# Weights split on GpSimd in narrower pieces, and one small product of a differential attention moved out of its loop

## The chip, the cores and the metric

The kernel runs on one core of a Trainium2 chip. The metric is the device time of one execution in microseconds (us). A core has five engines that work beside each other: TensorE (PE in the profile, its weight loads PEld), VectorE (DVE), ScalarE (ACT), GpSimd (POOL) and SyncE (SP), which here only issues DMAs. They meet through semaphores. SBUF is the memory on the chip that all of them use; PSUM is where PE writes its products.

## The reference

Four transformer layers run over 512 tokens of width 1024, batch 1, in float32: two of a first model (sparse attention with a convolution, then latent attention, each followed by an MLP of width 4096) and two of a second (a differential attention that also sees 256 context tokens, then an attention over a neighbourhood). Two things of it matter here. Every layer multiplies activations by large weight matrices (`h @ w_in`, `h @ w1` and so on). And the differential attention subtracts two softmaxes and normalises what comes out:

```python
    s = jnp.einsum('bqnd,bknd->bnqk', q, k).astype(F32) * scale
    p = jax.nn.softmax(s, axis=-1)
    p = p.reshape(bsz, n2 // 2, 2, nq, nk)
    w = p[:, :, 0] - lam * p[:, :, 1]
    o = jnp.einsum('bhqk,bkhe->bqhe', w.astype(v.dtype), v)
    ...
    o = rms_norm(o, subln_g) * (1.0 - lam_init)      # rms_norm adds EPS to the mean square
    (o.reshape(bsz, n, D_INNER) * jax.nn.silu(z)) @ w_out
```

## The kernel before

**Products in two parts.** PE multiplies in a float32 format of fewer bits (fp32r). To keep the reference's precision, each operand x is split into a rounded high part and the rest, x = hi + lo, and a product is three matmuls: hi x hi, hi x lo, lo x hi (`mm3`, lines 583, 584, 585). High parts are made by ACT (a copy into the rounded format), low parts by a subtraction on DVE or POOL (`sub_lo`, line 414, for activations).

**The stream of weights.** `WeightStream` passes all weights through SBUF in one order that `plan()` fixes: 355 units, most of them 128 partitions x 1024 columns, made of four blocks of 256 columns (`tm`, token-major products) or eight of 128 (`fmm`, feature-major). A block is what one step of the sum over the inner dimension uses. SP loads a unit into one of three raw buffers (line 264); `split` lets ACT make its high part (line 277) and POOL its low part (line 278) in one instruction each; a ring holds four split units. `tick` splits the next unit when the ring has room, and it is called after each group of products, so the order of the splits among POOL's other work is the order in which the program is written. Five units are split on DVE (`eng`). A matmul waits for the parts that it reads; an engine does its instructions in the written order.

**What else DVE and POOL do.** In the attentions, DVE turns scores in PSUM into masked scores with their extreme (L725, L2052, L2221), ACT exponentiates them into SBUF and sums each row, DVE divides (L735 in the causal attentions, L2232 in the neighbourhood attention), PE transposes the result. In layer 0 DVE also sums the index scores (L923). During the MLPs DVE forms the second model's modulation vector by long sums (L1267, `macc`). POOL makes low parts of activations (`hl`, L414), rotary products (L1701 to L1712), the gates (L1770) and, from its own queue, DMAs that copy the keys to the other 64 partitions (L1803).

**The differential attention** (`diff_run`) goes over 96 units (group of heads g, pair p, token tile t): 8 x 2 x 6. Unit by unit, one step apart: A forms two score tiles on PE; B adds the shift on DVE; E exponentiates on ACT, and each sum of a row lands in a small tile (`df_s0`, `df_s1`); Dm on DVE forms the factor of the second softmax, -lam x sum0 / sum1 (a reciprocal, L2072, and L2073), adds the second to the first (L2074) and writes EPS x sum0 squared into column t of the tile `oe` (L2077), for the softmaxes stay undivided and the norm's EPS must be scaled to match. T transposes, G multiplies by the values, and once for the six tiles of a pair Hn adds that column to the mean squares (L2111) and takes the root. The weight products of the next group run between these steps, with their splits.

Of the kernel before, what the change touches and what calls it, by code (L numbers as in the profile page):

```python
# [12 lines left out]
F32 = mybir.dt.float32  # L13
# [3 lines left out]
OP = mybir.AluOpType  # L17
# [8 lines left out]
EPS = 1e-6  # L26
# [220 lines left out]
class WeightStream:  # L247
# [20 lines left out]
    def split(s, eng=None):  # L268
        nc = s.nc
        u = s.halved  # L270
        s.load(u)
        key, nb, n = s.units[u]
        m = nb * n
        raw = s.raw.pop(u)
        hi = s.hi_pool.tile([128, UNIT], F32R, name="w_hi")
        lo = s.lo_pool.tile([128, UNIT], F32R, name="w_lo")
        nc.scalar.copy(hi[:, :m], raw[:, :m])  # L277
        (eng or nc.gpsimd).tensor_tensor(lo[:, :m], raw[:, :m], hi.bitcast(F32)[:, :m], OP.subtract)  # L278
        s.t[u] = lo, hi
        s.halved += 1  # L280
        s.load(u + s.ahead)
# [19 lines left out]
class Next:  # L301
    """Normalised input of a layer, feature-major in two parts, filled a pair of token tiles at a time."""

# [53 lines left out]
    def flush(s, n=4):  # L357
        """n of the four parts of the oldest pair's transposes."""
        parts = s.pend[0][1]
        for _ in range(min(n, len(parts))):  # L360
            parts.pop(0)()
        if not parts:
            s.pend.pop(0)
# [15 lines left out]
class Net:  # L379
# [22 lines left out]
    def psum(s, mm, tp=2, sp=0, s2=0):  # L402
        """The PSUM pools in force; a further call replaces them."""
        s.pctx.close()
        for n, b in (("tp", tp), ("mm", mm), ("sp", sp), ("s2", s2)):
            if b:
                setattr(s, n, s.pool_in(s.pctx, f"ps_{n}", b, space=PSUM))
# [179 lines left out]
    def tm(s, ps, units, xh, xl, tok, n, ks=range(8)):  # L587
        """Eight blocks of a token-major product, or those of ks."""
        blocks = [(u, b) for u in units for b in range(u[0].shape[1])]
        t = slice(tok, tok + 128)  # L590
        for k in ks:
            (wh, wl), b = blocks[k]
            s.mm3(ps, xh[:, k, t], xl[:, k, t], wh[:, b, :n], wl[:, b, :n], k == 0, k == 7)

    def fmm(s, ps, units, xh, xl, tok, n, c0=0, m=128, ks=range(8)):
        """The same with the features on the partitions."""
        blocks = [(u, b) for u in units for b in range(u[0].shape[1])]
        for k in ks:
            (wh, wl), b = blocks[k]
            s.mm3(ps, wh[:, b, c0:c0 + m], wl[:, b, c0:c0 + m], xh[:, k, tok:tok + n], xl[:, k, tok:tok + n], k == 0, k == 7)  # L600
# [10 lines left out]
    def rows_gemm(s, keys, lhs, evac, tail, npair, flush, wide_first=False, mid=None, k_first=False):  # L611
        """Token-major product over four 256-column chunks; the last two go pair of tiles by pair of tiles."""
        nc = s.nc
# [22 lines left out]
        def pair(i, c, us, free, between):  # L636
            """Two tiles, one weight unit after the other; the first unit is given back early where it is free."""
            ps = [s.mm.tile([128, 512], F32, name="mm")[:, :256] for _ in range(2)]
# [68 lines left out]
    def causal(s, units, qk, scale, mask, vs, pt, out, P, tmp, ofs, wide, fill, extra=lambda t: None):  # L707
        """Causal attention over (head, query tile) units; fill[t] holds the pieces of other work run in step t."""
        nc = s.nc
# [367 lines left out]
    def out_proj(s, name, order, lhs, M, ssp, rowt, sqp, make, gain, part=None, late=None):  # L1077
        """part: the first chunk's sum over the first unit, already formed."""
        nc = s.nc
# [501 lines left out]
    def tables2(s, pool, tmp):  # L1581
        """Rotary tables with the head gains folded in, the difference's factor and the output gain."""
        nc, io = s.nc, s.io
# [36 lines left out]
    def second(s, L, nx):  # L1620
# [135 lines left out]
        def gates_at(ts, g, chunks):  # L1756
            """z / (1 + exp(-z)), 128 columns at a time."""
            e = {}
# [254 lines left out]
    def diff_run(s, c):  # L2013
# [41 lines left out]
        def E(u):  # L2055
            g, p, t = u
            x = d[u]
            for j in range(2):
# [3 lines left out]
                ei[0] += 1  # L2062
                sm = s.sml.tile([128, 1], F32, name=f"df_s{j}")
                s.act(e, S, AF.Exp, bias=x["nb"][j], scale=-1.0, acc=sm)
                x["e"].append((e, sm))

        def Dm(u):
# [4 lines left out]
            nc.vector.reciprocal(rb, sb)  # L2072
            nc.vector.scalar_tensor_tensor(rb, sa, nlam, rb, OP.mult, OP.mult)  # L2073
            nc.vector.scalar_tensor_tensor(ea, eb, rb, ea, OP.mult, OP.add)  # L2074
            if t == 0:
                O[g, p] = ob.tile([128, 6, 128], F32, name="ob"), ob.tile([128, 6], F32, name="oss"), ob.tile([128, 6], F32, name="oe")
            nc.vector.scalar_tensor_tensor(O[g, p][2][:, t:t + 1], sa, EPS, sa, OP.mult, OP.mult)  # L2077

# [29 lines left out]
        def Hn(g, p):  # L2108
            o, ss, oe = O[g, p]
            v, y, a = [s.sml.tile([128, 6], F32, name=f"df_{k}") for k in "vya"]  # L2110
            nc.vector.scalar_tensor_tensor(v, ss, 1.0 / 128, oe, OP.mult, OP.add)  # L2111
            s.act(y, v, AF.Ln)
# [212 lines left out]
```

## Time and profile before

| | us |
|---|---|
| median of 3 runs | 3266.62 (3265.22 to 3267.99) |
| span of the profiled execution | 3260.0 |
| median of the runs over that span | 6.6 |
| PE busy | 3097.0 (95%) |
| DVE busy | 2143.7 (66%) |
| ACT busy | 1626.6 (50%) |
| POOL busy | 1527.3 (47%) |

The profile is of one execution. Its span goes from the first to the last instruction; the timed runs hold a few microseconds more around it. Busy time is the union of an engine's instructions. Durations are in us unless marked ns. An instruction that is held after it was issued shows a longer duration; one that waits for a semaphore shows idle time before it, and the profile names what ended that.

### The profile page before, as it was taken

The numbers are of one execution on the slowest core, as the hardware profiler recorded it, in microseconds if no ns is written. First come the engines' busy times: TensorE is split into PE (matmuls) and PEld (weight loads), VectorE is DVE, ScalarE is ACT, GpSimd is POOL, SyncE is SP. The second block draws the span as 40 slices with busy tenths as digits, with TensorE's granted clock in tenths as the row PEclk, the third lists the DMA queues.
The fourth block names the chain that finished last, engine by engine and source line by source line (L and its number), as shares of the span: only waits on it lengthen the run. The fifth ranks groups of instructions, "written<-read, shape, count | busy, mean of one in ns | idle before, by whom it ended". The sixth has DMA issues, their size and how long they took to land.

```text
span 3260.0 us, 59267 instructions
## 1 busy us (share of the span) xinstructions
PE 3097.0 (95%) x23124; PEld 2910.2 (89%) x23124; DVE 2143.7 (66%) x4332; ACT 1626.6 (50%) x3923; POOL 1527.3 (47%) x1344
## 2 busy tenths in 40 slices
PE   7999999998899999999999999998999999999889
PEld 7888889887788889889999999988999999999888
DVE  4885434466865354657777777778446777777775
ACT  4544533345765333455555555555235565555552
POOL 3433344434333444474654465443354554545544
PEclk9999999999999999999999999999999999999999
DMA  3122334432123343331222222212422323222324
GB/s 120 59 72 74 108 123 143 136 99 85 36 85 111 123 135 125 116 98 50 63 60 62 61 66 58 69 53 87 152 87 78 88 79 84 78 71 79 90 87 136
DMA packets 91012, 292.30 MB, mean 90 GB/s; under 512 B 18142, under 2 KB 23390, under 8 KB 87660
## 3 DMA queue, kind: packets, MB, share of 16 engines
q1 hardware_dynamic: 84028, 259.33, 24.7%
q0 software_dynamic: 5120, 25.17, 3.6%
q10 hardware_dynamic: 1584, 4.00, 0.4%
q8 instruction: 183, 3.00, 0.4%
q14 instruction: 97, 0.79, 0.1%
HBM read 244.38 MB, written 18.92 MB: 81 GB/s over the span
## 4 chain that ended last, share of the span: by engine, by line
PE 49%; DVE 11%; ACT 5%; issue 4%; POOL 3%; DMA 2%; SPq 0%; POOLq 0%; DVEq 0%; ACTq 0%
PE mm L583 12%; PE mm L585 12%; PE mm L584 12%; PE mm L2102 2%; ACT X L411 2%; POOL w_lo L278 2%; DMA KL<-KL 1%; PE s L2205 1%; PE tp L2244 1%; PE tp L2089 1%; PE mm L2259 1%; DVE s L2052 1%; PE mm L2253 1%; PE s L2206 1%; DVE X L735 1%
## 5 line engine op out<-in xcount | busy, mean ns | idle before, releaser
L278 POOL TENSOR_TENSOR w_lo<-w_raw,w_hi 128x1024 fp32r<-128x1024 f32 (+2 forms) x350 | 880.6, 2520 | 1033.8 <-ACT w_hi L277 1007.8
L583 PE MATMUL mm<-w_hi,hh 128*128 128x256 f32 (+3 forms) x2880 | 836.8, 291 | 7.8 <-ACT w_hi L277 2.5
L584 PE MATMUL mm<-w_lo,hh 128*128 128x256 f32 (+3 forms) x2880 | 817.0, 284 | 11.8 <-POOL w_lo L278 11.7
L585 PE MATMUL mm<-w_hi,hl 128*128 128x256 f32 (+3 forms) x2880 | 818.6, 284 | 2.8 <-POOL hl L414 2.4
L584 PEld LDWEIGHTS mm<-w_lo,hh 128*128 128x128 f32 x2880 | 548.0, 190 | 15.7 <-POOL w_lo L278 14.4
L583 PEld LDWEIGHTS mm<-w_hi,hh 128*128 128x128 f32 x2880 | 547.4, 190 | 16.0 <-ACT df_sq L411 8.5
L585 PEld LDWEIGHTS mm<-w_hi,hl 128*128 128x128 f32 x2880 | 546.2, 190 | 6.4 <-POOL hl L414 5.5
L277 ACT CAST w_hi<-w_raw 128x1024 fp32r<-128x1024 f32 (+2 forms) x355 | 366.5, 1036 | 206.0 <-PE mm L585 171.2
L583 PE MATMUL mm<-hh,w_hi 128*128 128x256 f32 (+1 forms) x1408 | 455.4, 323 | 3.0 <-DVE M L1088 2.8
L584 PE MATMUL mm<-hl,w_hi 128*128 128x256 f32 (+1 forms) x1408 | 448.2, 318 | 0.6
L585 PE MATMUL mm<-hh,w_lo 128*128 128x256 f32 (+1 forms) x1408 | 447.1, 318 | 1.2 <-DVE w_lo L278 1.2
L583 PEld LDWEIGHTS mm<-hh,w_hi 128*128 128x128 f32 x1408 | 266.0, 189 | 29.8 <-issue 5.2
L584 PE MATMUL mm<-w_lo,gh 128*128 128x256 f32 x1024 | 287.1, 280 | 1.4 <-POOL w_lo L278 1.4
L583 PE MATMUL mm<-w_hi,gh 128*128 128x256 f32 x1024 | 287.6, 281 | 0.0
L585 PE MATMUL mm<-w_hi,gl 128*128 128x256 f32 x1024 | 287.1, 280 | 0.1
L585 PEld LDWEIGHTS mm<-hh,w_lo 128*128 128x128 f32 x1408 | 265.7, 189 | 22.0 <-DVE w_lo L278 1.6
L584 PEld LDWEIGHTS mm<-hl,w_hi 128*128 128x128 f32 x1408 | 266.1, 189 | 21.3 <-DVE hl L345 1.7
L1267 DVE SCALAR_TENSOR_TENSOR macc<-modw,cg,macc 128x1024 f32<-128x1024 f32 x84 | 201.3, 2440 | 29.2 <-DMA modw<-in_mod 29.2
L584 PEld LDWEIGHTS mm<-w_lo,gh 128*128 128x128 f32 x1024 | 193.0, 188 | 1.9 <-POOL w_lo L278 1.6
L583 PEld LDWEIGHTS mm<-w_hi,gh 128*128 128x128 f32 x1024 | 193.2, 189 | 0.4
L585 PEld LDWEIGHTS mm<-w_hi,gl 128*128 128x128 f32 x1024 | 193.0, 188 | 0.5 <-DVE gl L414 0.5
L414 DVE TENSOR_TENSOR gl<-rsq,gh 128x512 fp32r<-128x512 f32 x64 | 45.6, 712 | 220.6 <-ACT gh L411 220.6
(372 smaller groups left out, 7089.0 us busy)
## 6 DMA issues: line engine op xcount, KB each, us to landing
w_raw<-in_w SPq DMA_DIRECT2D x336, 512.0 KB, 3.5
modw<-in_mod SPq DMA_DIRECT2D x24, 1024.0 KB, 5.8
KH<-KH POOLq DMA_DIRECT2D x32, 384.0 KB, 4.0
KL<-KL POOLq DMA_DIRECT2D x32, 384.0 KB, 5.0
xs<-X SPq DMA_DIRECT2D x12, 512.0 KB, 3.6
X<-xs SPq DMA_DIRECT2D x12, 512.0 KB, 6.7
yd<-ob SPq DMA_DIRECT2D x16, 384.0 KB, 2.3
X<-in_rpb SPq DMA_DIRECT2D x32, 192.0 KB, 3.7
```

What stands on the lines that cost most here:

```text
L277: nc.scalar.copy(hi[:, :m], raw[:, :m])
L278: (eng or nc.gpsimd).tensor_tensor(lo[:, :m], raw[:, :m], hi.bitcast(F32)[:, :m], OP.subtract)
L411: return s.nc.scalar.activation(out, in_, func, bias=bias, scale=scale, **kw)
L414: (eng or s.nc.vector).tensor_tensor(lo, x, hi.bitcast(F32), OP.subtract)
L583: mm(ps, ah, bh, start=first, stop=False)
L584: mm(ps, ah, bl, start=False, stop=False)
L585: mm(ps, al, bh, start=False, stop=last)
L735: nc.vector.tensor_scalar(d["P"][:, :d["n"]], d["P"][:, :d["n"]], rs, None, OP.mult)
L1267: nc.vector.scalar_tensor_tensor(acc[:, v], w[:, k2], cv, acc[:, v], OP.mult, OP.add)
L2052: nc.vector.tensor_tensor_reduce(S, S, s.zero.to_broadcast(list(S.shape)), nrq[:, h:h + 1], 3e38, OP.add, OP.min, nb)
L2089: nc.tensor.transpose(pt[:, k], ea[:, (k0 + k) * 128:(k0 + k + 1) * 128], s.ident)
L2102: nc.tensor.matmul(ps, x["w"][:, k], V[g][:, kb, p * 128:(p + 1) * 128], start=k == 0, stop=k == nk - 1)
```

## The change

The low half of a unit is made by POOL in several instructions of at least 256 columns each, whole blocks at a time: four for a unit of 4 x 256 or 8 x 128 columns, four of 276 for those of 1104. Units that DVE splits stay in one instruction.

In the differential attention the sum of the first softmax is written by ACT straight into column t of `oe`, which is allocated at the first exponential of a pair. L2077 leaves the loop; Hn squares all six columns and multiplies them by EPS in one instruction. The factor L2073 is formed by a tensor_scalar with two per-partition factors in place of a scalar_tensor_tensor. (Some docstrings became empty lines.)

```diff
@@ WeightStream.split
         nc.scalar.copy(hi[:, :m], raw[:, :m])
-        (eng or nc.gpsimd).tensor_tensor(lo[:, :m], raw[:, :m], hi.bitcast(F32)[:, :m], OP.subtract)
+        w = m if eng else n * max(1, 256 // n)
+        for c in range(0, m, w):
+            c = slice(c, min(m, c + w))
+            (eng or nc.gpsimd).tensor_tensor(lo[:, c], raw[:, c], hi.bitcast(F32)[:, c], OP.subtract)
@@ diff_run, E
-                sm = s.sml.tile([128, 1], F32, name=f"df_s{j}")
+                if j == 0 and t == 0:
+                    O[g, p] = ob.tile([128, 6, 128], F32, name="ob"), ob.tile([128, 6], F32, name="oss"), ob.tile([128, 6], F32, name="oe")
+                sm = s.sml.tile([128, 1], F32, name="df_s") if j else O[g, p][2][:, t:t + 1]
                 s.act(e, S, AF.Exp, bias=x["nb"][j], scale=-1.0, acc=sm)
@@ diff_run, Dm
             nc.vector.reciprocal(rb, sb)
-            nc.vector.scalar_tensor_tensor(rb, sa, nlam, rb, OP.mult, OP.mult)
+            nc.vector.tensor_scalar(rb, sa, rb, nlam, OP.mult, OP.mult)
             nc.vector.scalar_tensor_tensor(ea, eb, rb, ea, OP.mult, OP.add)
-            if t == 0:
-                O[g, p] = ob.tile([128, 6, 128], F32, name="ob"), ob.tile([128, 6], F32, name="oss"), ob.tile([128, 6], F32, name="oe")
-            nc.vector.scalar_tensor_tensor(O[g, p][2][:, t:t + 1], sa, EPS, sa, OP.mult, OP.mult)
@@ diff_run, Hn
+            nc.vector.scalar_tensor_tensor(oe, oe, EPS, oe, OP.mult, OP.mult)
             nc.vector.scalar_tensor_tensor(v, ss, 1.0 / 128, oe, OP.mult, OP.add)
```

## Rows read from the trace of the kernel before

**Rows 1.** The page: busy time by engine; the chain that ended last.

```profile
PE 3097.0 (95%) x23124; PEld 2910.2 (89%) x23124; DVE 2143.7 (66%) x4332; ACT 1626.6 (50%) x3923; POOL 1527.3 (47%) x1344
...
PE 49%; DVE 11%; ACT 5%; issue 4%; POOL 3%; DMA 2%; SPq 0%; POOLq 0%; DVEq 0%; ACTq 0%
```

**Rows 2.** Waits of PE: who waited for whom, us, times, longest.

```profile
PE s L2205 <- ACT X L411: 26.9, 39, 3.0
PE tp L743 <- DVE X L735: 20.2, 26, 1.5
...
PE mm L584 <- POOL w_lo L278: 13.1, 11, 2.2
PE tp L2244 <- DVE X L2232: 8.7, 5, 2.3
```

**Rows 3.** The core's span and its mean granted TensorE clock.

```profile
core 0: 3260.0 us, clock 0.991
```

**Rows 4.** POOL by line and shape: count; busy, mean ns; idle before.

```profile
L278 POOL TENSOR_TENSOR w_lo<-w_raw,w_hi 128x1024 fp32r<-128x1024 f32 x332 | 843.8, 2546 | 945.6 <-ACT w_hi L277 938.3 <-issue 2.5 <-PE tp L905 2.0
...
L1712 POOL TENSOR_TENSOR st<-X,X 128x256 f32<-128x256 f32 x64 | 47.8, 747 | 5.0
```

**Rows 5.** Timeline, 1386 to 1392.5: start, us, engine, line; idle time before.

```profile
1387.08 0.19 PEld L585 LDWEIGHTS mm<-w_hi,hl 128*128 128x128 f32 x1 [0.28 <-POOL hl L414]
...
1387.86 2.36 POOL L278 TENSOR_TENSOR w_lo<-w_raw,w_hi 128x1024 fp32r<-128x1024 f32 x1
...
1387.96 0.19 PEld L585 LDWEIGHTS mm<-w_hi,hl 128*128 128x128 f32 x1 [0.46 <-POOL hl L414]
...
1390.17 2.81 POOL L414 TENSOR_TENSOR hl<-nf_f,hh 128x256 fp32r<-128x256 f32 x4
...
1390.27 0.58 PE L584 MATMUL mm<-w_lo,hh 128*128 128x256 f32 x1 [1.50 <-POOL w_lo L278]
```

**Rows 6.** Two lines of DVE: ns minimum/median/maximum, first and last start.

```profile
L2077 DVE SCALAR_TENSOR_TENSOR oe<-df_s x96: 145/154/2392, 1459.8 to 2285.2; 128x1 f32<-128x1 f32 x96
...
L2232 DVE TENSOR_SCALAR X<-X,na_r x128: 486/554/2677, 2477.5 to 3185.5; 128x512 f32<-128x512 f32 x64, 128x640 f32<-128x640 f32 x64
```

**Rows 7.** DVE by line and shape: count; busy, mean ns; idle before.

```profile
L2052 DVE CUSTOM_DVE_ANT_0 s<-s,zero,nrq 128x768 f32<-128x768 f32 x128 | 127.3, 1022 | 3.9 <-PE s L2042 2.6
...
L2077 DVE SCALAR_TENSOR_TENSOR oe<-df_s 128x1 f32<-128x1 f32 x96 | 66.6, 693 | 0.0
...
L2073 DVE SCALAR_TENSOR_TENSOR df_rb<-df_s,nlam,df_rb 128x1 f32<-128x1 f32 x96 | 44.1, 459 | 3.5
...
L2072 DVE RECIPROCAL df_rb<-df_s 128x1 f32<-128x1 f32 x96 | 13.4, 140 | 97.9 <-ACT X L411 97.8
```

**Rows 8.** Timeline, 1671.5 to 1675.2: DVE and POOL in the differential attention.

```profile
1671.53 2.76 POOL L278 TENSOR_TENSOR w_lo<-w_raw,w_hi 128x1024 fp32r<-128x1024 f32 x1 [0.57 <-ACT w_hi L277]
...
1671.94 2.37 DVE L2077 SCALAR_TENSOR_TENSOR oe<-df_s 128x1 f32<-128x1 f32 x1
...
1674.24 0.47 POOL L1770 TENSOR_TENSOR SZ<-SZ,ge 128x128 f32<-128x128 f32 x1
```

**Rows 9.** Timeline, 3183 to 3189: POOL, DVE and PE in the neighbourhood attention.

```profile
3185.43 2.35 POOL L278 TENSOR_TENSOR w_lo<-w_raw,w_hi 128x1024 fp32r<-128x1024 f32 x1 [3.21 <-ACT w_hi L277]
...
3185.52 2.54 DVE L2232 TENSOR_SCALAR X<-X,na_r 128x512 f32<-128x512 f32 x1
...
3187.73 0.64 POOL L1770 TENSOR_TENSOR SZ<-SZ,ge 128x128 f32<-128x128 f32 x1
3188.20 0.63 PE L2244 MATMUL tp<-ident,X 128*128 128x128 f32 x4 [2.33 <-DVE X L2232]
```

**Rows 10.** Timeline, 404 to 411: DVE's long sums and a low half.

```profile
405.28 4.62 DVE L1267 SCALAR_TENSOR_TENSOR macc<-modw,cg,macc 128x1024 f32<-128x1024 f32 x2
...
405.66 3.17 POOL L278 TENSOR_TENSOR w_lo<-w_raw,w_hi 128x1024 fp32r<-128x1024 f32 x1 [2.84 <-ACT w_hi L277]
```

**Rows 11.** Timeline, 107 to 112: a DVE sum of layer 0.

```profile
108.82 2.19 DVE L923 SCALAR_TENSOR_TENSOR am<-relu,wi,am 128x384 f32<-128x384 f32 x1 [0.25 <-ACT relu L411]
```

## The prediction

> **What bounds the kernel now.** I read the page first. TensorE (PE) is busy 3097.0 of the 3260.0 us span, so it is the bound, and a change can only pay through the 163 us in which PE stands, or by making PE stand more [rows 1]. VectorE (DVE) holds 11% of the chain that ended last and POOL 3% [rows 1]: most of what PE waits for is made on DVE, little of it directly on POOL. The view of PE's waits then says where: behind DVE's softmax scalings (L735 20.2 us, L2232 8.7), behind exponentials that follow a DVE reduction (L2205, 26.9), and 13.1 us in 11 waits directly for a low half w_lo made on POOL [rows 2]. These are many short waits, none of them over 3.0 us in these rows. PE also lost a little to its clock: the mean granted clock is 0.991 [rows 3], so 0.009 x 3260 = 29 us of full-clock work was not granted. That time stands at the lower of the two levels (1.2 GHz) and comes after PE has stood.
>
> **POOL's cost of the pieces.** 332 of the 350 low halves are one instruction over 1024 columns, 2546 ns on average; 256 columns take 747 [rows 4]. So each instruction has a fixed part: (2546 - 747) / 768 = 2.34 ns a column leaves 747 - 256 x 2.34 = 148 ns. Behind one another, four instructions of 256 columns, of the same operation, took 2.81 us together [rows 5], against 2.36 for the whole unit just ahead of them. So each unit costs POOL 0.45 us more, 332 x 0.45 = 149 us, and POOL goes from 1527.3 us, 47% of the span [rows 1], to some 51%. It stays far from full. The low half in pieces is still one tile, but its readers need not wait for all of it: in rows 5 the tile hl is written by four POOL instructions, and PE waits for them one at a time (0.28 and 0.46 us at L585). I take it that w_lo is tracked the same way.
>
> **What the pieces free: DVE.** Many DVE instructions run far over their usual time, and the small ones tell why. L2077 works on one column and takes 154 ns at the median but 2392 at worst [rows 6], 693 on average [rows 7]. At 1671.94 it took 2.37 us: POOL had begun a w_lo at 1671.53, and L2077 ended as that w_lo did; the next POOL instruction was already issued at 1674.24 and cost its usual 0.47 [rows 8]. The same at 3185.52: L2232 (median of its line 554 ns) took 2.54 us behind the w_lo of 3185.43, and PE, which needed its result, stood 2.33 us [rows 9]. There DVE got in between two POOL instructions that followed one another: L1770 took 0.64 instead of 0.47 because DVE went first. L2052, which reads PSUM, took 1022 ns on average [rows 7] and shows no such holds. So a DVE instruction that reads or writes SBUF in this way waits for the end of the POOL instruction that is running, and POOL waits for DVE in turn: a w_lo that found DVE busy took 3.17 us [rows 10], and the second of two DVE sums then stood behind it, 4.62 us for both; it ended 1.1 us after the w_lo (405.28 + 4.62 - 405.66 - 3.17), about what one sum takes.
>
> With pieces DVE waits for the end of a piece, not of a unit. Each L2232 or L735 caught at the start of a unit waits up to 0.75 us, not 2.4. For the case in rows 9: the first piece would end 0.75 us after 3185.43, so DVE is done 1.6 us earlier, and PE's 2.33 us shrink to some 0.8.
>
> For the sum I followed every PE delay over 60 ns back (what released it, what that had waited for or stood behind on its engine, to the last matmul). The trail of 88 of them leads through 66 DVE instructions held by a w_lo; the first is L923 at 108.82 [rows 11], the last the L2232 of rows 9. Counting for each the shorter of PE's delay and the hold gives 48.5 us. Putting the end of the next piece (some 0.75 us after the start of the unit, then every 0.70, 2.81 / 4) in place of the unit's end leaves holds that give back 39.8 us of it. That is a ceiling for the step: the next DVE instruction of the same trail can be held again by the next piece (POOL goes first when DVE's next one follows directly, rows 10), and behind a shortened hold something else is late next, such as the exponential on ACT. I take 60%, **-24 us**; ends -48 and -5.
>
> In the multilayer perceptrons DVE's long sums (rows 10) gain nothing: two sums with a piece ahead of each wait no less in all than with one unit ahead of one of them once pieces and sums alternate, and POOL's unit grows to some 5 us (2.81 and two sums). PE does not stand there, so I cost it at zero; it would show as waits for w_lo if the four units in stock ran out.
>
> **The direct waits for w_lo.** In rows 5 PE stood 1.50 us for a w_lo of 2.36. Its first quarter would be there 1.6 us earlier, but the last 0.45 us later, and PE needs one quarter every 0.4 us (three products, at 3097.0 us for 23124 [rows 1] 0.13 us each) while POOL makes one in 0.7. PE would start early and then wait at each quarter, and the four blocks end about 0.5 us earlier. Eleven such waits: **-5 us**, ends -13 and +4.
>
> **What POOL's longer units delay.** Behind them in POOL's queue stand the gate products (L1770), the rotary products, the hl splits of the next layer (rows 5) and the two copies of the keys per group, issued from that queue. Each may start 0.45 us later. PE waits little for them, since 163 us of waits name them hardly [rows 2]; I charge ten places at 0.5: **+5 us**, ends 0 and +27 (the 3% of the chain that is POOL's, 98 us, stretched by 0.45/2.36 = 19%, gives +19; with DVE going first between pieces some +27).
>
> **The differential attention.** L2077 goes: 96 instructions, 66.6 us of DVE [rows 7], of which 96 x 0.154 = 15 us is work and the rest holds. Added are 16 instructions over six columns (as long as one column by their kind, 16 x 0.15 = 2.5 us). L2073 becomes one instruction with two per-partition factors. No row shows that form on one column: if it is never held and as short as L2072's reciprocals, 96 x (459 - 140) ns = 31 us of DVE go too; if it is held like L2073, nothing goes. I take the middle, as pieces shorten the hold to 0.25 either way. On PE nearly all of this is inside the 66 trails (12 go through L2077, 7 through L2073, about 9 us of delay together), since PE stands little in that stage; so 0 beside the -24, ends -4 and 0. The sum column that ACT now writes straight into the group's tile moves no instruction.
> The Trainium skill, SBUF — State Buffer, "Summary: rules for kernel authors", says that tensor_scalar can enter a mode that takes the pair of ports shared with GpSimd. By that rule the new factor is held as before; the sum would be 0 to 1 us higher. L2232, a tensor_scalar between SBUF tiles, agrees [rows 9]; for one column no run shows it.
>
> **Clock.** With a third of PE's stops shortened some of the stretches at the lower level should not come: **-3 us**, ends -12 and +3.
>
> **Sum** against the profiled execution: 3260.0 - 24 - 5 + 5 - 3 = 3233 us of span. The timed runs (median 3266.6) stand 6.6 us above that span, so 3240.
>
> **Rivals.**
> A, everything held comes free (48 + 13, 4 in the attention, 6 of clock, 5 lost): 3266.6 - 66 = 3201. For it: holds repeat group by group with the same length. Against: trails share later steps. With three quarters of it, 3217. Chance 0.12 for below 3222.
> B, the freed DVE time is off PE's path: other work is late next, a quarter of the ceiling is kept (-10) and POOL takes 6 back: 3262. For it: PE is already at 95%. Against: rows 9, where nothing stands between DVE and PE. Chance 0.14.
> C, slower: POOL becomes the late one where layers meet, around 1320 to 1440 us and 2400 to 2440, where PE already waits for w_lo behind hl splits [rows 5]. The 3% of the chain grows by 27 us with DVE let in between pieces, and DVE gives 8: 3286. It decides once a unit with its interruptions takes longer than PE needs for one. Against: POOL is idle half of the span. Chance 0.08.
> The Trainium skill, VectorE: DVE Perf Modes, "The TRN2 errata", advises tiles of 512 columns or more because each instruction pays a fixed part; it speaks of VectorE and ScalarE. It points to rival C; by rows 4 two pieces of 512 would cost POOL 0.15 us a unit and hold DVE 1.35 us at most.
> D, the change doesn't do what it says: POOL keeps going through its four pieces before DVE gets in. Then holds grow by 0.45 us, 66 x 0.3 = +20 less 4 in the attention: 3282. Against: rows 8 and 9. Chance 0.03.
>
> **Numbers.** Forecast 3240 with chance 0.63, its own range 3222 to 3256. 0.2% is 6.5 us, about what timing can tell from no change. The range 3214 to 3266 takes in most of A and B. Faster (below 3260): forecast, A and a third of B, 0.79; same: the rest of B and the top of the forecast's spread, 0.11; slower: C and D, 0.10.
>
> **What would show it.** Right: some 1370 POOL instructions on L281 of 0.7 us each; POOL busy near 1680 us (1527.3 and 149); the longest L2232 (then L2235) near 1.3 us instead of 2.68; DVE busy below 2000; PE's waits behind L735 and L2232 (then L738 and L2235) down by half; PE's busy time about the same and the span near 3233. Wrong: PE waits for w_lo above 13 us in total, holds on DVE still above 2 us, or DVE freed by 150 us with PE's waits unchanged.

## The result and the profile after

The change makes the kernel faster: 3242.5 us (median; 3240.7 to 3243.8) against 3267.3 before, ratio 0.9923, 95% interval 0.9909 to 0.9937. The forecast was 3240. The profiled execution took 3240.7 us with a span of 3238.6, where 3233 had been worked out. So a run stands some 2 us above its own span, as all runs on record do. Of the 6.6 us by which the sum went from span to time, the other 4.5 must come from the profiled execution of before having taken some 3262 us and not the median's 3266.6; so the span missed by 5.6 us where the time missed by 2.5, and two traces differ by 21.4 us where the medians differ by 24.8.

Busy time by engine and the chain that ended last, of the kernel after, as in [rows 1]:

```profile
PE 3097.3 (96%) x23124; PEld 2914.6 (90%) x23124; DVE 1930.0 (60%) x4252; ACT 1618.0 (50%) x3923; POOL 1741.3 (54%) x2376
...
PE 56%; DVE 6%; POOL 4%; ACT 4%; issue 3%; DMA 2%; SPq 0%; POOLq 0%; DVEq 0%; ACTq 0%
```

PE does the same work in the same busy time (3097.0 and 3097.3), so in sum the 21.4 us of span are time in which PE stood; stretch by stretch that is not so, as the tables below show. DVE lost 214 us and nearly half of its share of the chain; POOL gained as much, 214 us.

PE's waits after, as in [rows 2]:

```profile
PE s L2208 <- ACT X L414: 21.2, 33, 3.0
PE tp L746 <- DVE X L738: 16.0, 22, 1.5
...
PE mm L588 <- POOL hl L417: 5.6, 5, 2.3
PE mm L586 <- DVE ot L1957: 5.5, 3, 3.1
...
PE mm L587 <- POOL w_lo L281: 4.3, 11, 0.6
...
PE s L2044 <- DMA KH<-KH: 3.6, 1, 3.6
PE s L2208 <- DMA KH<-KH: 3.3, 1, 3.3
...
PE tp L2247 <- DVE X L2235: 1.5, 2, 0.8
```

The waits that the pieces were to shorten are shorter: 26.9 to 21.2, 20.2 to 16.0, 13.1 to 4.3 and 8.7 to 1.5 us. The forecast had L735 and L2232 together down by half; they went from 28.9 to 17.5, L735 by a fifth only. Four rows grew. In the kernel before they were:

```profile
PE mm L585 <- POOL hl L414: 2.4, 4, 1.0
...
PE s L2205 <- DMA KH<-KH: 2.2, 2, 2.0
...
PE mm L583 <- DVE ot L1954: 1.5, 2, 0.8
...
PE s L2041 <- DMA KH<-KH: 0.4, 1, 0.4
```

The growth behind hl and the copies of the keys (KH) has a place in the forecast, that behind the product's eviction L1957 (L1954 before) has none. The copy that PE's L2044 waited for is in layer 2 (near 1440 us), the one of L2208 in the last layer (near 3078 us).

What one hold became shows at the place of [rows 9]. POOL, DVE and PE in the timeline after:

```profile
3165.99 3.01 POOL L281 TENSOR_TENSOR w_lo<-w_raw,w_hi 128x256 fp32r<-128x256 f32 x4 [3.22 <-ACT w_hi L277]
...
3166.09 0.93 DVE L2235 TENSOR_SCALAR X<-X,na_r 128x512 f32<-128x512 f32 x1
...
3167.16 0.63 PE L2247 MATMUL tp<-ident,X 128*128 128x128 f32 x4 [0.70 <-DVE X L2235]
```

DVE comes in after the first of four pieces and is done in 0.93 us instead of 2.54; PE stands 0.70 us instead of 2.33. The forecast for this place was 1.6 us earlier and some 0.8.

POOL's pieces and two groups of DVE (by line and shape: count; busy, mean ns; idle before), and the minimum/median/maximum of the two lines that answer to [rows 6]:

```profile
L281 POOL TENSOR_TENSOR w_lo<-w_raw,w_hi 128x256 fp32r<-128x256 f32 x1336 | 1061.6, 826 | 802.3 <-ACT w_hi L277 780.2 <-PE mm L587 9.3 <-issue 5.6
...
L1270 DVE SCALAR_TENSOR_TENSOR macc<-modw,cg,macc 128x1024 f32<-128x1024 f32 x84 | 127.7, 1564 | 31.8 <-DMA modw<-in_mod 31.8
...
L2078 DVE TENSOR_SCALAR df_rb<-oe,df_rb,nlam x96: 272/273/276, 1450.7 to 2265.9; 128x1 f32<-128x1 f32 x96
...
L2235 DVE TENSOR_SCALAR X<-X,na_r x128: 485/554/1112, 2466.4 to 3166.1; 128x512 f32<-128x512 f32 x64, 128x640 f32<-128x640 f32 x64
```

A piece takes 826 ns on average, not the 700 of four undisturbed ones, since DVE gets in between. Four of them take 3.18 us (1061.6 / 334), against 843.8 / 332 = 2.54 for a whole unit in [rows 4]. So a unit costs POOL 0.64 us more and not 0.45; that is the difference between POOL's 1741 us and the 1680 of the forecast.

**Where along the program the time came from.** Both kernels issue 23124 matmuls in the same order, so the start of the n-th matmul can be subtracted between two traces. The table gives how much each kernel won (+) or lost on the kernel before in each stretch (bounds by the time of before, us). It also holds the experiments below.

```
             0-   320-  680-  900- 1340- 1400- 1480- 2280- 2360- 2480- 3080- 3160-   all
            320   680   900  1340  1400  1480  2280  2360  2480  3080  3160   end
after     +12.4  +0.4  -0.8  +2.2  -2.4  -3.9 +10.9  -5.9  -4.0 +11.5  -2.6  +3.7  +21.4
pieces    +11.1  +0.4  -0.9  +2.2  -2.4  -3.1 +10.1  -2.7  -4.1 +11.0  -4.5  +3.8  +20.7
attn       +1.6  +0.0  -0.6  +0.6  -0.2  +0.1  +7.8  -0.7  -0.0  +0.3  -0.5  +0.0   +8.5
meet whole +9.4  +0.4  -2.3  +2.3  -3.0  +0.7 +10.2  -0.3  -0.6 +10.9  -2.6  +3.7  +28.9
yraw ACT  +11.8  +0.4  -1.0  +2.3  -2.5  -3.9 +11.2  -5.9  -4.4 +11.1  -2.0  +2.6  +19.8
refill    +12.7  +0.4  -0.9  +2.3  -2.6  -3.5 +10.8  +1.7  +0.1 +12.2  -1.8  +3.7  +35.2
reversed   +8.5  -0.4  -0.1  +1.5  -3.9  -3.2 +11.0  -3.4  -4.4 +11.2  -4.6  +3.4  +15.6
512       +11.3  +0.2  -1.8  +1.6  -2.5  -2.9 +10.3  -2.9  +1.4 +11.2  -3.3  +2.7  +25.6
mlp whole +11.0  +0.1  +0.0  +1.9  -0.1  -5.2 +10.7  -5.6  -0.1 +10.7  -2.4  +3.4  +24.5
5th piece  +2.2  -1.1  -5.4  -1.1  -9.5 -10.2 +10.0  -7.7  -6.5  +0.6  -5.9  -3.0  -37.5
select     +9.7  +0.0  +2.2  +0.7  -0.2  -1.6  +9.9  -0.2  -0.7 +10.1  -5.0  +3.7  +28.6
sel 512   +11.3  +0.1  -0.2  +1.5  -0.6  +0.3  +9.1  -1.4  -2.2 +10.9  -2.8  +2.5  +28.4
sel no at  +8.7  +0.0  +2.5  +0.7  +0.8  +0.4  +9.2  +0.2  -3.1 +11.0  -1.5  +3.6  +32.5
```

Each row is one execution. Part of a row is time in which PE stood, the rest is PE's own busy time, which is longer where more of it ran at the lower clock. The second table takes PE's busy time out of both traces: by how much PE stood less (+) or more (-) than before in the same stretches, and the mean granted clock of a stretch in the two kernels.

```
             0-   320-  680-  900- 1340- 1400- 1480- 2280- 2360- 2480- 3080- 3160-   all
            320   680   900  1340  1400  1480  2280  2360  2480  3080  3160   end
after      +9.6  +0.3  +0.5  +1.0  -0.7  -3.0  +6.8  -4.0  -0.4  +9.9  -1.8  +3.6  +21.7
meet whole +9.1  +0.3  +0.8  +1.0  -0.8  +0.2  +4.9  -0.2  -0.6  +9.4  -2.5  +3.6  +25.3
refill     +9.9  +0.3  +0.6  +1.0  -0.9  -2.6  +6.8  +1.5  +0.2 +10.7  -1.9  +3.6  +29.1
reversed   +6.1  -0.2  +1.3  +0.4  -0.4  -2.1  +7.0  -3.0  -2.5  +9.7  -3.7  +3.5  +16.2
512        +9.9  +0.0  +0.2  +0.4  -0.2  -1.0  +6.6  -2.3  +0.3  +9.8  -1.0  +2.6  +25.5
mlp whole  +9.3  -0.0  -0.3  +0.6  +0.3  -3.0  +7.0  -3.0  +0.1  +9.0  -1.3  +3.3  +22.0
5th piece  +5.0  -1.0  -2.6  -1.4  -4.5  -6.8  +5.4  -4.8  -3.1  +1.4  -4.7  +1.2  -16.1
clock bef. 0.98  1.00  0.98  1.00  0.94  1.00  0.99  1.00  0.99  1.00  0.94  1.00  0.991
clock aft. 1.00  1.00  0.97  1.00  0.92  0.98  1.00  0.98  0.96  1.00  0.92  0.99  0.990
```

The change wins 41.1 us in six stretches and loses 19.6 us in the other six, 16.2 of them where one layer hands over to the next (1340 to 1480 and 2280 to 2480 us). That is twice the net result, and the experiments are about these two sums. PE's standing shows the same two sides, smaller: 31.7 us less in seven stretches, 9.9 us more in five, and in each of the five the clock also came out lower. So half of the loss, and a quarter of the gain, is PE's busy time. The five kernels with the same units before 320 us (after, pieces, meet whole, yraw ACT, refill) won from 9.4 to 12.7 us there, and stood less by 9.1 to 9.9: the standing repeats better than the total.

**Where the late transfers come from.** In the stretch 2280 to 2360 us PE waits for the product's eviction L1957, which on DVE stands behind the split of yraw, which waits for a load. SP's DMA issues, POOL and PE of the kernel after:

```profile
2319.76 1.52 SPq L1942 DMA_DIRECT2D yraw<-yd  x2
2325.44 4.39 SPq L264 DMA_DIRECT2D w_raw<-in_w  x2
2329.92 0.86 SPq L1942 DMA_DIRECT2D yraw<-yd  x2
...
2321.49 7.97 POOL L281 TENSOR_TENSOR w_lo<-w_raw,w_hi 128x256 fp32r<-128x256 f32 x8
...
2320.12 0.39 PE L586 MATMUL mm<-w_hi,hh 128*128 128x256 f32 x1 [2.07 <-DVE ot L1957]
2336.21 0.53 PE L586 MATMUL mm<-w_hi,yh 128*128 128x256 f32 x1 [3.09 <-DVE ot L1957]
```

The same place in the kernel before (18.7 us later on its clock):

```profile
2336.53 1.52 SPq L1939 DMA_DIRECT2D yraw<-yd  x2
2340.88 2.88 SPq L264 DMA_DIRECT2D w_raw<-in_w  x2
2344.24 1.99 SPq L1939 DMA_DIRECT2D yraw<-yd  x2
...
2338.27 5.13 POOL L278 TENSOR_TENSOR w_lo<-w_raw,w_hi 128x1024 fp32r<-128x1024 f32 x2
...
2350.53 0.39 PE L583 MATMUL mm<-w_hi,yh 128*128 128x256 f32 x1 [0.63 <-DVE ot L1954]
```

A load of w_raw needs a raw buffer, and a buffer is free when the unit in it has been split. Two units took POOL 5.13 us before and 7.97 after, with DVE's splits going in between. So the second load left SP only at some 2329.5 (the row of two that starts at 2325.44 ends at 2329.83), and the yraw load queued behind it left at 2329.92: 4.4 us later than the 2344.24 of before, set on the same clock (2344.24 - 18.7 = 2325.5). The 5.9 us lost in this stretch are 4.0 of standing and 1.9 of PE's busy time, at a granted clock of 0.98 instead of 1.00 after the stop of 3.09 us.

For the KH of layer 2 the queue is not the matter but, as I read it, the transfers beside it. Median issue to landing around the first group of layer 2, before (first fence) and after:

```profile
w_raw<-in_w SPq DMA_DIRECT2D x4, 512.0 KB, 3.8
KH<-KH POOLq DMA_DIRECT2D x2, 384.0 KB, 4.6
```

```profile
w_raw<-in_w SPq DMA_DIRECT2D x4, 512.0 KB, 6.3
KH<-KH POOLq DMA_DIRECT2D x2, 384.0 KB, 7.5
```

The first copy's issue before and after:

```profile
1445.14 0.75 POOL L1803 DMA_DIRECT2D KH<-KH  x1 [1.28 <-ACT KH L411]
```

```profile
1433.40 0.75 POOL L1806 DMA_DIRECT2D KH<-KH  x1
```

At this point the matmuls of the kernel after are 12.3 us ahead, so the copy left 0.6 us later against them (1433.40, and 1445.14 - 12.3 = 1432.84). And the group's two copies took 2.9 us longer at the median (7.5 and 4.6): the two loads of w_raw ahead of it had left SP 1.5 and 1.9 us later (at 1430.67 and 1433.48, before at 1441.51 and 1443.89), and the second ran together with it. That the load beside it is what slowed the copy is not shown by an experiment of its own; where the second load left some 1.3 us ahead of the copy again (meet whole and select), the first copy landed in 4.4 and 4.5 us.

### The profile page after: what moved, and what is told of

It reads as the page before. It is cut to its first block, busy times and chain, and to the rows that moved or that the text cites. A ratio compares the mean times of both kernels' runs of the same rounds, so it can differ in the third digit from the quotient of the medians.

```text
span 3238.6 us, 60338 instructions
## 1 busy us (share of the span) xinstructions
PE 3097.3 (96%) x23124; PEld 2914.6 (90%) x23124; DVE 1930.0 (60%) x4252; ACT 1618.0 (50%) x3923; POOL 1741.3 (54%) x2376
## 4 chain that ended last, share of the span: by engine, by line
PE 56%; DVE 6%; POOL 4%; ACT 4%; issue 3%; DMA 2%; SPq 0%; POOLq 0%; DVEq 0%; ACTq 0%
PE mm L586 14%; PE mm L588 14%; PE mm L587 14%; PE mm L2104 3%; POOL w_lo L281 3%; PE tp L2091 2%; PE s L2044 1%; DMA KL<-KL 1%; PE s L2045 1%; PE s L2208 1%; ACT X L414 1%; PE tp L2247 1%; PE mm L2262 1%; PE s L2209 1%; PE mm L2256 1%
## 5 line engine op out<-in xcount | busy, mean ns | idle before, releaser
L281 POOL TENSOR_TENSOR w_lo<-w_raw,w_hi 128x256 fp32r<-128x256 f32 (+2 forms) x1382 | 1100.6, 828 | 876.2 <-ACT w_hi L277 836.4
L2055 DVE CUSTOM_DVE_ANT_0 s<-s,zero,nrq 128x768 f32<-128x768 f32 (+1 forms) x192 | 158.7, 844 | 18.4 <-PE s L2045 15.7
```

The lines of the kernel that those rows point to most:

```text
L281: (eng or nc.gpsimd).tensor_tensor(lo[:, c], raw[:, c], hi.bitcast(F32)[:, c], OP.subtract)
L2055: nc.vector.tensor_tensor_reduce(S, S, s.zero.to_broadcast(list(S.shape)), nrq[:, h:h + 1], 3e38, OP.add, OP.min, nb)
```

## Experiments

Ratios are to the kernel before, run beside each. The change itself stands at 0.9923 (0.9909 to 0.9937), so a kernel differs from it surely only where the intervals part.

**The two parts alone.** First the pieces without the attention's edits, then these with whole units:

```diff
-        (eng or nc.gpsimd).tensor_tensor(lo[:, :m], raw[:, :m], ...)
+        w = m if eng else n * max(1, 256 // n)
+        for c in range(0, m, w): ...
```

> The kernel before with the pieces of 256 columns and nothing else of the change. Theory P (nearly all of the gain is the shorter holds): 3240 to 3246 us against 3267 before and 3242 for the whole change; L2077 (one column) stays but its mean falls from 693 ns to some 250. Rival Q (the attention's part carries a share of its own, the 9 us of PE delay that was traced through L2077 and L2073): some 3250 us. In both the four places where the changed kernel loses against the kernel before (near 1370, 1450, 2340 and 2465 us) lose again if the pieces make them.

> The kernel before with the differential attention's part alone, whole units of 1024 columns on POOL. Theory P: 3263 us (4 us less than 3267, at most 9, all between 1450 and 2250 us), the new factor's instruction still up to 2.4 us long at worst because a whole unit holds it. Rival Q: 3258 us. Neither expects a loss near 2340 or 2465 us, which the pieces are to make.

Measured: the pieces 3241.6 us, 0.9932 (0.9917 to 0.9947), as good as the whole change. The attention's part 3257.7 us, 0.9978 (0.9968 to 0.9988): 7 us (4 to 10 by the interval), nearer Q's 9 than P's 4. (The traced execution took 3253.3 us, so its total in the table is some 4 us high.) The pieces lose again at all four places near 1370, 1450, 2340 and 2465 us (-2.4, -3.1, -2.7 and -4.1), the attention's part at none (-0.7 at most): the pieces make these losses. P holds for the pieces, Q for the attention alone, and the parts don't add: between 1480 and 2280 us they win 10.1 and 7.8 us alone and 10.9 together. They remove the same stops: PE's waits there behind DVE's splits of the keys and queries (KL, QS) were 6.7 us before and are 1.4, 2.1 and 1.1 us with the pieces, the attention's part and both. The new factor's instruction in the kernel with whole units, and in the pieces alone the two lines that it replaces:

```profile
L2075 DVE TENSOR_SCALAR df_rb<-oe,df_rb,nlam x96: 272/273/277, 1457.0 to 2275.1; 128x1 f32<-128x1 f32 x96
```

```profile
L2080 DVE SCALAR_TENSOR_TENSOR oe<-df_s x96: 147/154/705, 1452.5 to 2267.9; 128x1 f32<-128x1 f32 x96
...
L2076 DVE SCALAR_TENSOR_TENSOR df_rb<-df_s,nlam,df_rb x96: 219/291/1573, 1451.3 to 2267.2; 128x1 f32<-128x1 f32 x96
```

The one instruction with two factors is never held, even by whole units (277 ns at most), where P expected up to 2.4 us. L2080 is the L2077 of before, which took 2392 ns at worst in [rows 6]; with pieces it takes 705, one piece. Its mean fell from 693 to 375 ns, not to the 250 that P expected.

**Whole units where layers meet.**

```diff
-        w = m if eng else ...
+        w = m if eng or 199 <= u < 203 or 259 <= u < 283 else ...
```

> The whole change, but 28 of 355 units are again formed in one instruction: v2:0, q2:1, all of o2 and all of layer 3 up to q3:1, those that POOL forms between 1417 and 1440 and between 2200 and 2460 us. Theory M: a unit in pieces is done 0.45 us later, or up to 2.8 us for two where DVE gets in between, so its raw buffer is free later, the next load of w_raw is issued later on SP, and it collides there with the copies KH and KL (PE waited 3.6 and 3.3 us for KH) or holds up the yraw loads queued behind it (PE waited 3.1 us behind L1957). Then three places that lost 4.4, 5.9 and 4.0 us are won back: 3242 - 14 = 3228 us, at worst half of it, 3235. Rival N: those losses come from DVE's new order or from the lower clock after a chance stop, and stay: 3240 to 3245.

Measured: 3235.7 us, 0.9912 (0.9894 to 0.9931). The timing alone doesn't part it from the change, but the table does at the places: 1400 to 1480 from -3.9 to +0.7, 2280 to 2360 from -5.9 to -0.3, 2360 to 2480 from -4.0 to -0.6. PE's waits there, 1425 to 1480 us (one row) and 2290 to 2350:

```profile
PE s L2044 <- DMA KH<-KH: 0.4, 1, 0.4
...
PE mm L586 <- DVE ot L1957: 1.6, 2, 1.1
```

The wait for KH is back at the 0.4 us that it had in the kernel before, and L1957 at 1.6 (1.5 before). So M holds for the first two places and N falls there. At the third N is nearer: PE stood no less there than in the change (-0.6 and -0.4), and what came back is PE's busy time, at a granted clock of 0.99 instead of 0.96. The 3228 of M was not reached, and 3235.7 lies at its worst bound. In the trace the three places give 13.6 us, as M has it, but other stretches take 6 back; between 0 and 320 us, with the same units, that is PE's busy time (9.4 won against 12.4, while it stood less by 9.1 against 9.6).

**The yraw loads off SP's queue.** First all of them on ACT's queue, then only the refills:

```diff
-            nc.sync.dma_start(yt[b], yd[8 + b])
+            nc.scalar.dma_start(yt[b], yd[8 + b])                           # yraw ACT
+            (nc.sync if b < NY else nc.scalar).dma_start(yt[b], yd[8 + b])  # refill
```

> The whole change, with the yraw loads of the output projections (line 1942) issued from ACT's queue instead of SP's, so they no longer stand behind the loads of w_raw. Theory M: the 3.1 and 2.1 us that PE waited behind L1957 near 2320 to 2340 us go, the waits for KH stay: 3242 - 5 = 3237 us. Rival R (POOL's late w_lo or DVE itself is what PE waits for at L1957, not the transfer): 3242 us, with L417 of yl as late as before.

> The whole change with only the refills of yraw on ACT's queue; the first two loads of layer 2 stay on SP, so the gate loads on ACT's queue keep their place ahead. Theory M: the stops of 2.1 and 3.1 us behind L1957 near 2320 and 2336 us go and no new one comes for the gates (5.7 us when all yraw loads were on ACT's queue): 3242 - 5 = 3237 us. Rival R (the late yraw loads are a sign, not the cause): 3242 us.

Measured: 3241.9 us, 0.9931 (0.9915 to 0.9948), and for the refills alone 3235.2 us, 0.9889 (0.9874 to 0.9905), whose interval just parts from that of the change. (The traced execution took 3226.8 us, so its total in the table is some 8 us high.) The first kernel had no wait for L1957 left between 2330 and 2342 us, but a new one earlier. PE's wait there and DVE's row that caused it:

```profile
PE mm L586 <- DVE ot L1957: 5.7, 1, 5.7
```

```profile
2308.83 0.76 DVE L1957 TENSOR_TENSOR ot<-mm,gate 128x256 f32<-128x256 f32 x2 [15.57 <-DMA gate<-ed]
```

The first two yraw loads had gone ahead of the gates in ACT's queue: an equal stop in another place. With only the refills moved, POOL is as slow as in the change and PE doesn't stand:

```profile
2317.81 7.60 POOL L281 TENSOR_TENSOR w_lo<-w_raw,w_hi 128x256 fp32r<-128x256 f32 x8 [3.47 <-ACT w_hi L277]
```

So PE's stop in this stretch comes by SP's queue and not by POOL's lateness itself. The stretch goes from -5.9 to +1.7 (M expected 5 us). The next goes from -4.0 to +0.1, though its units are still in pieces. PE's waits there are nearly the same, though (it stood 0.4 us more than before in the change and 0.2 less here): the loss of 4.0 us in the change is nearly all PE's busy time, and its clock of 0.96 is 0.99 here. Why the clock fell in the one and not in the other was not tried.

**POOL slower by one more piece a unit.**

```diff
-        for c in range(0, m, w):
+        for c in [*range(0, m, w)] + ([] if eng else [(m - 1) // w * w]):
```

> The whole change with the last piece of each unit on POOL formed twice, so each unit takes POOL 0.70 us longer (POOL's busy time 1741 to some 1985 us) and no hold gets longer. Theory M (what the pieces cost is that a unit is done later, and with it its raw buffer and the next load): the places near 1450, 2340 and 2465 us lose two and a half times what they do now (14 us for 0.45 a unit), so some 20 us more, 3262 us; at least 3250. Rival N (POOL has half of its time to spare, the losses there are of another kind): 3242 to 3246 us.

Measured: 3297.1 us, 1.0103 (1.0085 to 1.0120), slower than before. Its busy times, and two of PE's waits with the core's span and clock:

```profile
PE 3118.4 (95%) x23124; PEld 2930.7 (89%) x23124; DVE 1952.3 (59%) x4252; ACT 1619.5 (49%) x3923; POOL 2014.3 (61%) x2726
```

```profile
PE mm L587 <- POOL w_lo L281: 15.8, 28, 1.4
...
PE s L2209 <- DMA KL<-KL: 11.7, 8, 3.7
...
core 0: 3297.6 us, clock 0.983
```

N falls: a fifth piece in each unit cost 59 us of span (3297.6 against 3238.6) with POOL busy for 61% of it, far more than M's 20. It took POOL 273 us more, not 244. No piece is wider, but DVE meets more of them: its busy time is up by 22 us, so a share of the loss may be holds and not lateness. The loss is also wider than M had it: 10 us before 320, 11 between 2480 and 3080 us. PE stood 38 us longer, and its busy time is 21 us longer at a mean granted clock of 0.983 instead of 0.990: after the added stops PE ran more often at the lower level. Only the stretch 1480 to 2280 us is as in the change (+10.0).

**The early start.**

```diff
-        for c in range(0, m, w):
+        for c in reversed(range(0, m, w)):
```

> The whole change with the four pieces of each unit formed in reverse, so the block that PE reads first is formed last. DVE's holds and POOL's load stay as they are; only the early start of PE goes. Theory S (the early start is worth what the direct waits fell by): PE waits for w_lo rise from 6 us in the changed kernel to some 18 (13.1 in 11 waits before, and 0.45 for each), so 3242 + 12 = 3254 us. Rival T (PE arrives when the whole unit is long done nearly everywhere, and what it wins at the first block it loses at the next): 3242 to 3246 us.

Measured: 3246.3 us, 0.9940 (0.9923 to 0.9956). PE waits for w_lo as S has it:

```profile
PE mm L587 <- POOL w_lo L281: 19.6, 15, 2.8
```

That is 15.3 us more, but the span grew by only 5.8 (21.4 - 15.6 in the table). S is right on the waits and wrong on the span; T's time fits, though not its reason. The intervals of the two kernels overlap, so only the traces tell these 5.8 us. That PE, once late, finds later things ready is my reading of it and was not tested.

**Pieces of 512.**

```diff
+        w = m if eng else n * max(1, 512 // n)
```

> The whole change with pieces of 512 columns, two a unit. A hold lasts at most 1.3 us instead of 0.75 (2.4 for whole units), a unit costs POOL 0.15 us more instead of 0.45. Theory M (two effects: the holds, worth some 35 us outside the places where layers meet, and the late raw buffers there, worth 14): about 60% of the one and a third of the other, 35 x 0.6 - 5 = 16 less than before, 3250 us. Rival N (the hold's length matters little once DVE gets in at all, and POOL's fixed part is the price): 3235 us.

Measured: 3239.2 us, 0.9921 (0.9905 to 0.9938), the same as the change within the interval. M is wrong in its 60%: the six winning stretches give 37.3 of 41.1 us, and in the seven where the change stands less PE stands less by 29.5 of 31.7. N's reason holds: of the longer holds little reaches PE, and in the other five it stands longer by 4.2 us instead of 9.9. POOL's pieces, and PE's waits for the two softmax scalings, which were 16.0 and 1.5 us with 256 columns:

```profile
L281 POOL TENSOR_TENSOR w_lo<-w_raw,w_hi 128x512 fp32r<-128x512 f32 x668 | 952.4, 1449 | 870.5 <-ACT w_hi L277 847.5 <-PE mm L587 10.5 <-issue 6.1
...
PE tp L746 <- DVE X L738: 17.7, 23, 1.5
...
PE tp L2247 <- DVE X L2235: 2.3, 3, 1.2
```

**The perceptrons whole.**

```diff
+        w = m if eng or key[0] == "w" else n * max(1, 256 // n)
```

> The whole change, but the 128 units of the two multilayer perceptrons (w1, w2) whole again. Theory P (there the pieces free DVE and not PE): 3242 us within 3, though DVE's sums L1270 go back from 1564 ns to some 2440 on average (84 of them, 74 us of DVE). Rival U (the freed DVE time is worth something there): 3250 us or more, with waits of PE behind L1270 or for w_lo in the stretches 330 to 700 and 900 to 1340 us.

Measured: 3237.6 us, 0.9919 (0.9901 to 0.9936), the same as the change. P holds: DVE's sums are back at their old length and PE loses 0.6 us in the two stretches of the perceptrons.

```profile
L1270 DVE SCALAR_TENSOR_TENSOR macc<-modw,cg,macc 128x1024 f32<-128x1024 f32 x84 | 201.6, 2444 | 29.0 <-DMA modw<-in_mod 29.0
```

It doesn't lose where the second perceptron ends (1340 to 1400: -0.1 against -2.4), whose last units are whole here; 1.0 us of that is standing, the rest PE's busy time. It also doesn't lose between 2360 and 2480 us (-0.1 against -4.0), where its units are those of the change. There PE waited 1.5 us for KH at the layer's first score product (L2208), and in the change 1.2 us at the same product; so the copies of the keys are not what the change loses there, its clock is (0.96 against 0.99).

**The selection.** Whole units in the perceptrons and where layers meet, pieces elsewhere; then with 512 columns, then without the attention's part.

```diff
+        w = m if eng or key[0] == "w" or 199 <= u < 203 or 259 <= u < 283 else n * max(1, 256 // n)
```

> The whole change with pieces of 256 columns only where they paid: the 128 units of the perceptrons and the 28 where layers meet are whole. Theory M (the losses are local and add up): the places near 1390 (4.8 us), 1450 (4.4), 2340 (5.9) and 2465 us (4.0) are all free of loss, 3242 - 19 = 3223 us. Theory V (parts of what is won back at one place are lost at the next, so the two measured gains of 6.7 and 4.8 us are an upper bound): 3231 to 3236 us.

> The same selection with two pieces of 512 columns in the units that stay cut. Theory H (a hold up to 1.3 us is hidden by what PE has in hand, only longer ones reach it, as the pieces of 512 gained 3239 us against 3242): as fast as the selection with 256 within 3 us. Rival K (at equal places the shorter hold is worth more, and 512 was only as fast because it lost less where layers meet): 6 to 10 us slower than the selection with 256.

> The selection with 256 columns without the differential attention's part. Theory O (both parts take away the same stops between 1480 and 2280 us, 9 us with the pieces and 8 us without them, so beside pieces the attention's part is worth nothing): within 2 us of the selection with it. Rival A (the part keeps its own 7 us): 7 us slower.

Measured: 3230.8 us, 0.9879 (0.9863 to 0.9895); 3233.4 us, 0.9886 (0.9870 to 0.9901); 3232.3 us, 0.9883 (0.9869 to 0.9898). The selection beats both kernels, the change by 12 us in the medians and 14 by the ratios. M's four places are free of most of their loss (-0.2, -1.6, -0.2, -0.7), but 0 to 320 and 3080 to 3160 us come out lower than in the change, so V is right on the size. H and O hold: neither 256 instead of 512 nor the attention's part can be told from nothing here. The refills on ACT's queue and the selection were not tried together.

## Why the prediction was right, step by step

The time was right. Of the terms, the holds and the direct waits came out close to their sizes, POOL's longer units were charged too little, and the clock had the wrong sign. In the traces PE stands 21.7 us less, where -24 - 5 + 5 = -24 had been worked out, and its busy time is 0.3 us longer, where the clock was to give 3: that is the 5.6 us by which the span missed. In the timed runs the forecast gain of 27 us was 24.8; that the time came closer than the span is the luck of which execution of before was profiled.

- **Holds, -24 (ends -48 and -5): about right.** PE stands 31.7 us less in seven stretches. With the pieces reversed it is 27.8 there, so the early start has some 4 of it and the shorter holds some 27 to 28, two thirds of the ceiling of 39.8 where I took 60%. Losses in the same stretches are already taken off, so this is a net figure. The reason that I gave for the missing part, that the next piece holds DVE again, was not tested. The pieces of 512 show another side of it: with holds cut only to half, PE still stands 29.5 of the 31.7 us less. My reading is that what DVE's results have in hand before PE needs them covers most of a hold of one piece.
- **Direct waits, -5: right.** They fell from 13.1 to 4.3 us with PE waiting quarter by quarter (11 waits, 0.6 at most), and the early start is worth 5.8 us of span by the reversed pieces.
- **POOL's longer units, +5 (ends 0 and +27): mis-sized.** PE stands 9.9 us longer in the five stretches that lose by it. The step that was too small is what can stand behind a late unit: I counted POOL's own queue. That part is there: the waits behind hl grew by 3.2 us (2.4 to 5.6). The larger part came through the raw buffer: a later split frees it later, the next load leaves SP later, holds up yraw behind it (4.0 us, shown by the refills) and runs beside KH in layer 2 (a wait of 3.6 us, back to 0.4 with whole units there). And a unit grew by 0.64 us on average, not 0.45, and by more where DVE got in often: 7.97 us for two. By the totals of the first table the loss is 19.6 us, but the other half of it is PE's busy time and belongs to the clock. The stretch 3080 to 3160 (PE stands 1.8 us more, of it 1.3 for KH) was not traced by an experiment of its own.
- **The differential attention, 0 beside the pieces: right.** The pieces alone are as fast as the whole change, with and without the selection. Alone it is worth 7 us where I had traced 9 us of delay. The factor's instruction lies between my ends (459 and 140 ns) at 273. The Trainium skill, SBUF — State Buffer, "Who interferes with whom" (the prediction names another section of that page), lists tensor_scalar among the operations that can take the pair of ports shared with GpSimd. For one column with two factors the runs show no hold (272 to 277 ns), while L2235 at 512 columns is still held (1112 ns at most, 554 at the median).
- **Perceptrons, 0: right for PE, wrong for DVE.** I wrote that the sums gain nothing. They fell from 2.44 us each on average (2.31 in [rows 10]) to 1.56, since a sum now meets one piece and not a unit; PE hardly notices (it stands 0.3 and 1.0 us less in the two stretches).
- **Clock, -3: wrong in sign.** The mean granted clock went from 0.991 to 0.990 [rows 3], 29 to 32 us not granted. It is not one small sum but two larger ones: the first stretch, in which PE stood less, ran at 1.00 instead of 0.98, and the places where layers meet ran lower (0.94 to 0.92, 1.00 to 0.98, 1.00 to 0.98, 0.99 to 0.96), in layer 2 and near 2336 us right after the new stops of 3.6 and 3.1 us.

Of the rivals, A falls: even in the stretches that won PE's standing shrank by 31.7 us, half of the 61 that A has for holds and waits. C was right on the place: POOL was late where layers meet, and the fifth piece shows a kernel 1% slower than before. Not in C was the road, through SP's queue and the transfers. B and D are refuted by the tables and by L2235's maximum of 1112 ns. The advice that stood beside C, 512 columns or more (the Trainium skill, VectorE: DVE Perf Modes, "The TRN2 errata"), costs and gives nothing that the runs can tell here: 0.9921 against 0.9923.

## What to carry to other kernels

When an instruction on an engine that shares something with another is cut up, the hold gets shorter and the engine slower, and both show: look for the second where the cut engine gives a buffer back, and at what is queued behind the load that waits for this buffer. Cut only where a hold reaches the bound engine, and no finer than what that engine has in hand. Two edits that free the same stop don't add, so each is worth measuring alone and on top of the other. And when a loss is read off two traces, take PE's standing and its busy time apart first: here half of what looked like late transfers was PE's clock, part of it in the wake of those stops.

## What the runs showed of the hardware

- DVE and POOL alternate between short instructions: a piece of 256 columns averages 826 ns over the program against some 700 in a row undisturbed (2.81 us for four, [rows 5]), and two units took 7.97 us where DVE's splits came in between.
- A DVE tensor_scalar with two per-partition factors over one column is not held by POOL (272 to 277 ns in 96), unlike scalar_tensor_tensor over one column (up to 2392 ns, [rows 6]).
- Two copies of 384 KB issued from POOL's queue landed in 4.6 us at the median when the second of two loads of 512 KB had left 1.2 us ahead of the first copy, and in 7.5 us when it left at the same time.
- A load that waits on SP's queue for a buffer holds up the load queued behind it: yraw left 4.4 us late behind one load of w_raw, and on ACT's queue PE's stop behind it was gone.
- PE's clock followed its stops: after a stop of 3.6 us the stretch 1400 to 1480 us ran at a mean of 0.98 instead of 1.00, and a kernel with 59 us more of span had 21 of them as longer busy time, at 0.983 instead of 0.990. But nearly the same stops (2360 to 2480 us) came with 0.96 in the change and 0.99 with the refills moved.
